# A two-layer hybrid trunk: TensorE keeps the order of the source over the sixteen RWKV units

## The chip, the core and the metric

The kernel runs on one core of a Trainium2 chip. A core has five engines, each with a queue of its own that it works off in order: TensorE (PE in the tables, its weight loads PEld), VectorE (DVE), ScalarE (ACT), GpSimd (POOL) and SyncE (SP), which issues most of the DMAs. The metric is the device time of one execution in microseconds. The kernel before took 1853.83 us, the median of three runs (1851.74, 1853.83 and 1856.85).

## The reference

One step of a trunk with two layers over 128 context tokens and 256 latent tokens, 384 in all, of width 1024, in float32. Layer 0 mixes with a Mamba-2 (SSD) head group beside an RWKV-7 head group, layer 1 with gated linear attention beside an mLSTM group. A squared-ReLU MLP follows each. What matters here is layer 0: one input projection feeds both groups, and RWKV-7 scans each of 16 heads in two directions:

```
s_kk = einsum('bhvk,bhk->bhv', s, kk_t)
s = s * exp(lw_t)[:, :, None, :] - s_kk[..., None] * (kk_t * a_t)[:, :, None, :] + v_t[..., None] * k_t[:, :, None, :]
y = einsum('bhvk,bhk->bhv', s, r_t)
...
out = concatenate([y_ssd, y_rw], axis=-1) @ p['w_out']
```

The kernel computes this scan by chunks of 64 tokens: per chunk a triangular 64x64 matrix is inverted, and a chain over the chunks carries the state.

## The kernel before, in words

**Units and slots.** Two heads share the 128 partitions (64 rows each), so there are eight pairs of heads, and with two directions sixteen RWKV units. `ab_streams` (line 1527) runs through 19 slots `s`. In slot `s` the unit `s` is prepared (`rw_prep`: the product `psc` of `KR` and `BK`, six matmuls at a time; and once per pair `rw_shared`: `pn`, `pw`, `pa`, `pst`), unit `s-1` is inverted (`rw_tokmajor` with `pv`, `pbk` and the product named `pr` that reads `UV,Q`, then `rw_inverse`), and unit `s-2` runs its chain (`rw_chain`: four rounds of `pr` <- `S,KR`, then `pu`, then `pd` and `py`). Beside them run the SSD head group's steps (`aux`) and the fill: the dense input projection (`dps`, three float32r matmuls per 128 rows of weights, split into a high part `wH` by ACT and a low part `wL` by DVE) and pieces of the conditioning map (`mod`, four matmuls that each use 32 columns of the array, so that four fit beside each other).

**Round trips.** A matmul writes PSUM; ACT or DVE brings the result to SBUF; only then can a next matmul read it. `rw_inverse` (line 1279) is a string of such trips: five times `pz`, then ACT copies it to `Zb`, then `pw` and `pt` read `Zb`, then DVE makes the new `W` and `T` from them, then the next `pz` reads `T`. At the end `pe` reads the last `T`, a last `pt` transposes `T`, ACT copies that to `W`, and `pc` reads it. `rw_chain` (line 1373) has `pr`, DVE `R`, `pu`, ACT and DVE `UV`, `pd`, DVE `S`, and again `pr`.

**What sets the order.** Each of these parts is a Python generator that yields where a round trip begins. `run` (line 1584) draws them in turn by a share of steps done, so the source order already lays other work between the two ends of a trip: a fill step is two blocks of 128 rows, six `dps` matmuls. That source order was then only a priority. A scheduler went over the whole program with its own idea of how long each instruction takes, and put next on each engine the first instruction, by source order, that it held to be ready. Where it held the next matmul in source order not to be ready, it took a later one instead.

**PSUM.** `dps` and `aux` have one bank each in this loop, the preparation's tiles and `mod` share two banks in turn, the inverse has two, the chain one, and `py` one.

Names that the change and the rows touch: line 221 issues every matmul, line 1266 the transposes `pbk`, lines 235 and 239 DVE's operations, line 277 ACT's copies.

Of the kernel before, what the change touches and what calls it, by code (L numbers as in the profile page):

```python
# [175 lines left out]
class Net:  # L176
# [1350 lines left out]
    def ab_streams(self):  # L1527

        NB = 16
        sh, us, fills = self.sh, self.us, self.fills  # L1530
        st = [dict() for _ in range(NB)]
        py = {}
        self.steps.update({"set": 7, "fill0": 37, "fill1": 24, "fill2": 15, "fill3": 14, "fill14": 16, "fill15": 32, "fill16": 30,
                           "fill17": 29, "ssd1": 11, "ssd2": 6, "ssd3": 9, "prep0": 12, "prep1": 9, "inv": 17, "tail": 3})
        for s in range(NB + 3):
            self.one_acc = s < NB
            self.lpool = LPOOL.get(s, 0)
            if s == 1:

                row = lambda: self.mpool.tile([128, T], F32, tag="nt", name="prow", bufs=2)[:, 0:128]  # L1540
                self.params_tr(self.params_in(range(3, self.params.shape[1] // 128), row, self.nc.sync))
            streams = []
            b = s - 2
            if 0 <= b < NB:
                j, d = divmod(b, 2)
                if d == 0:
                    py[j] = self.psy.tile([128, 512], F32, tag="y", name="py")
                streams.append(("chain", self.rw_chain(j, d, st[b], py[j], sh[j])))
            b = s - 1
            if 0 <= b < NB:  # L1550
                streams.append(("inv", self.seq(self.rw_tokmajor(b % 2, sh[b // 2], st[b]), self.rw_inverse(b % 2, st[b]))))
            b = s
            if b < NB:
                j, d = divmod(b, 2)
                prep = self.rw_prep(j, d, sh[j], st[b])
                if d == 0:
                    streams.append(("prep0", self.seq(self.rw_shared(j, sh[j]), prep)))
                else:
                    streams.append(("prep1", self.seq(prep, self.rw_bonus(j, sh[j]))))
            if s >= 4 and s % 2 == 0 and (s - 4) // 2 < 8:  # L1560
                j = (s - 4) // 2
                streams.insert(0, ("tail", self.rw_tail(j, sh[j], sh[j]["y"])))
            q, g = s % 4, s // 4
            if s < NB and q:
                if q == 1:
                    core = self.ssd_core(g, us[g])
                streams.append(("ssd%d" % q, self.part(core, SSD_PARTS[q])))
            if s == 0:
                streams.append(("set", self.set))
            if fills[s]:  # L1570
                streams.append(("fill%d" % (q if 0 < s < NB - 2 else s), self.pipe(fills[s])))
            self.run(streams)
        return sh[7]["y"]

    def part(self, gen, n):
# [1004 lines left out]
```

## Time and profile before

| | |
|---|---|
| device time, three runs | 1851.74, 1853.83, 1856.85 us |
| profiled execution | 1853.32 us, of it 1851.2 us from the first to the last instruction |
| PE busy | 1765.5 us (95%), 13661 matmul records |
| PEld busy | 1480.9 us (80%) |
| DVE busy | 1301.8 us (70%) |
| ACT busy | 1069.6 us (58%) |
| mean granted TensorE clock | 0.98 of 2.4 GHz |

The loop in question takes the stretch from about 88 us to 870 us. The first chain reaches its state output (`pf`) at 175 us and the sixteenth at 828 us, so fifteen units lie in 652.8 us. A float32 matmul shows as two records in the trace, a float32r or float16 matmul as one. A matmul's row tells start and duration, but matmuls overlap in the array, so what one costs is read from its start to the start of the next. Rows of one kind that follow each other are merged, with their number behind an x.

### The profile page before, as it was taken

How to read it: one execution, taken by the hardware profiler on the slowest of the kernel's cores; microseconds unless marked ns; L12 is line 12 of the kernel's file. 1: busy time of each engine (PE TensorE's matmuls, PEld its weight loads, DVE VectorE, ACT ScalarE, POOL GpSimd, SP SyncE). 2: the span in 40 equal slices, each digit the busy share in tenths (PEclk: the TensorE clock that was granted, in tenths of full speed). 3: DMA queues.
4: the chain of work that ended last, by engine and by line, in shares of the span. 5: the costliest groups of instructions: out<-in, count | busy, mean ns of one | idle time of the engine just before them, and what ended most of it. 6: DMA issues, size and time to landing. Idle time of an engine off the chain costs nothing.

```text
span 1851.2 us, 37384 instructions
## 1 busy us (share of the span) xinstructions
PE 1765.5 (95%) x13661; PEld 1480.9 (80%) x13661; DVE 1301.8 (70%) x2992; ACT 1069.6 (58%) x2688; POOL 216.6 (12%) x270
## 2 busy tenths in 40 slices
PE   7879999999999999999999999899999998999998
PEld 3667767766666677786999998889989897999887
DVE  3698788777878889758766334786786958766434
ACT  3567475746574777646655333777676756755322
POOL 3222111110112011101000000020211212000000
PEclk9889999999999999999999999999999998999999
DMA  8332443333334322345445643333333233344432
GB/s 280 112 88 65 123 133 97 106 87 112 102 105 126 101 65 81 100 119 175 117 124 171 177 146 101 102 91 102 102 94 92 74 108 106 115 125 126 150 134 80
DMA packets 314107, 213.55 MB, mean 115 GB/s; under 512 B 39648, under 2 KB 297494, under 8 KB 313924
## 3 DMA queue, kind: packets, MB, share of 16 engines
q1 hardware_dynamic: 308756, 208.35, 38.6%
q10 hardware_dynamic: 4816, 2.69, 0.5%
q8 instruction: 107, 1.75, 0.4%
q14 instruction: 76, 0.62, 0.1%
q0 software_dynamic: 352, 0.13, 0.0%
HBM read 201.32 MB, written 9.78 MB: 114 GB/s over the span
## 4 chain that ended last, share of the span: by engine, by line
PE 75%; DVE 10%; ACT 8%; DMA 4%; issue 2%; POOL 1%; SPq 0%; DVEq 0%; ACTq 0%; POOLq 0%
PE dps L221 45%; PE o L221 7%; PE ps L221 4%; PE mod L221 3%; PE aux L221 2%; DVE wL L235 2%; PE psc L221 2%; DMA raw<-in_w_mod 2%; PE py L221 1%; PE pt L221 1%; DVE cacc L242 1%; PE pr L221 1%; ACT wH L277 1%; PE pw L221 1%; ACT Zb L277 1%
## 5 line engine op out<-in xcount | busy, mean ns | idle before, releaser
L277 ACT ACTIVATE wH<-raw 128x256 fp32r<-128x256 f32 (+1 forms) x790 | 363.3, 480 | 429.3 <-PE dps L221 309.6
L235 DVE TENSOR_TENSOR wL<-raw,wH 128x256 fp32r<-128x256 f32 (+2 forms) x771 | 398.9, 536 | 243.2 <-ACT wH L277 239.5
L277 ACT ACTIVATE Zb<-pz 64x384 f16<-64x384 f32 x160 | 77.2, 483 | 36.4 <-PE pz L221 34.1
L242 DVE SCALAR_TENSOR_TENSOR cacc<-rows,params,cacc 128x384 f32<-128x384 f32 (+1 forms) x192 | 94.2, 491 | 0.7
L221 PE MATMUL dps<-sH,wH 128*128 128x384 f32 x232 | 85.8, 371 | 4.0 <-DVE m L235 3.5
L221 PE MATMUL dps<-sL,wH 128*128 128x384 f32 x232 | 80.5, 347 | 0.3 <-DVE sL L235 0.2
L221 PE MATMUL dps<-sH,wL 128*128 128x384 f32 x232 | 79.7, 345 | 0.5 <-DVE wL L235 0.5
L221 PE MATMUL dps<-h0H,wH 128*128 128x384 f32 (+1 forms) x147 | 58.9, 401 | 8.2 <-ACT h0H L277 3.5
L235 DVE TENSOR_TENSOR AO<-AHb,rwmask 128x768 f16<-128x768 f16 (+1 forms) x112 | 60.1, 537 | 7.7 <-PE pz L221 6.0
L235 POOL TENSOR_TENSOR BK<-BK,kkk 128x768 f32<-128x768 f32 x16 | 33.8, 2110 | 221.5 <-DVE BK L239 150.5
L221 PE MATMUL mod<-xT,cond 128*32 128x384 f32 (+1 forms) x320 | 55.2, 485 | 3.8 <-DVE Q L235 2.5
L221 PE MATMUL dps<-h6H,wH 128*128 128x384 f32 (+2 forms) x147 | 54.9, 373 | 2.7 <-ACT wH L277 2.7
L221 PE MATMUL dps<-h2H,wH 128*128 128x384 f32 (+1 forms) x147 | 55.6, 378 | 1.4 <-ACT wH L277 1.4
L221 PE MATMUL dps<-h4H,wH 128*128 128x384 f32 (+1 forms) x147 | 54.9, 378 | 2.1 <-ACT h4H L245 2.1
L235 POOL TENSOR_TENSOR gDb<-gb 128x384 f32<-128x384 f32 x28 | 33.2, 1187 | 173.5 <-DVE gb L2230 73.2
L221 PE MATMUL dps<-h1H,wH 128*128 128x384 f32 (+1 forms) x147 | 52.0, 354 | 0.0
L221 PE MATMUL dps<-h6H,wL 128*128 128x384 f32 (+2 forms) x147 | 50.8, 346 | 1.2 <-DVE wL L235 1.2
L221 PE MATMUL dps<-h0H,wL 128*128 128x384 f32 (+1 forms) x147 | 51.7, 351 | 0.0
L221 PE MATMUL dps<-h1H,wL 128*128 128x384 f32 (+1 forms) x147 | 51.6, 351 | 0.0
L221 PE MATMUL dps<-h0L,wH 128*128 128x384 f32 (+1 forms) x147 | 51.5, 356 | 0.0
L221 PE MATMUL dps<-h1L,wH 128*128 128x384 f32 (+1 forms) x147 | 51.3, 355 | 0.0
L221 PE MATMUL dps<-h2H,wL 128*128 128x384 f32 (+1 forms) x147 | 51.1, 348 | 0.0
(1163 smaller groups left out, 5450.0 us busy)
## 6 DMA issues: line engine op xcount, KB each, us to landing
raw<-in_w_mlp_up SPq DMA_DIRECT2D x64, 512.0 KB
raw<-in_w_mlp_down SPq DMA_DIRECT2D x64, 512.0 KB
raw<-in_w_in_ab SPq DMA_DIRECT2D x204, 128.0 KB
xT<-in_w_mod SPq DMA_DIRECT2D x128, 192.0 KB
raw<-in_w_in_cd SPq DMA_DIRECT2D x192, 128.0 KB
raw<-in_w_mod SPq DMA_DIRECT2D x64, 192.0 KB
raw<-in_w_mod SPq DMA_DIRECT2D x32, 256.0 KB
raw<-in_w_out_cd SPq DMA_DIRECT2D x64, 128.0 KB
```

What stands on the lines that cost most here:

```text
L221: self.nc.tensor.matmul(out, lhsT, rhs, start=start, stop=stop)
L235: return (eng or self.nc.vector).tensor_tensor(out=out, in0=a, in1=b, op=op)
L242: self.nc.vector.scalar_tensor_tensor(out=out, in0=a, scalar=s, in1=b, op0=op0, op1=op1)
L277: self.nc.scalar.activation(out=out, in_=in_, func=AF.Copy)
```

## The change

The call of `run` in `ab_streams` is put into a context in which the scheduler keeps TensorE's instructions in the order in which the source issues them. The other engines' instructions are still ordered by the scheduler, and so are TensorE's before and behind this loop. No instruction is added or taken away: both programs have 11552 matmuls and 2640 explicit weight loads.

```
             if fills[s]:
                 streams.append(("fill%d" % (q if 0 < s < NB - 2 else s), self.pipe(fills[s])))
-            self.run(streams)
+            with self.tc.manual_schedule(engines={mybir.EngineType.PE}):
+                self.run(streams)
         return sh[7]["y"]
```

What moves is shown at two places of slot 11. The first is TensorE before, from the end of a `pt` group of the inverse (before, this stretch ran at 596 to 603 us). `xT_9111` to `xT_9117` are the four pieces of one `mod` step.

```order
L221 MATMUL pr<-S,KR 64x64 x2
L221 MATMUL dps<-h0H,wL 128x384
L221 MATMUL dps<-h1H,wH 128x384
L221 MATMUL dps<-h1L,wH 128x384
L221 MATMUL mod<-xT_9111,cond 32x384
L221 MATMUL mod<-xT_9113,cond 32x384
L221 MATMUL pb<-t_9192,const_base 128x384
L221 MATMUL mod<-xT_9115,cond 32x384
L221 MATMUL dps<-h1H,wL 128x384
L221 MATMUL dps<-h2H,wH 128x384
L221 MATMUL dps<-h2L,wH 128x384
L221 MATMUL mod<-xT_9117,cond 32x384
```

TensorE in the changed kernel at the same place, behind the same `pt` group; the first `pz` is the next product of the inverse.

```order
L221 MATMUL pr<-S,KR 64x64 x2
L221 LDWEIGHTS AO_793
L221 MATMUL pz<-T,AO_793 128x64
...
L221 MATMUL mod<-xT_9146,cond 32x384
L221 MATMUL mod<-xT_9148,cond 32x384
L221 MATMUL mod<-xT_9150,cond 32x384
L221 MATMUL mod<-xT_9152,cond 32x384
L221 MATMUL pu<-R,WF 64x64 x2
```

The four `mod` now stand together, where before `pb` and `dps` stood between them. The ten `dps` that stood between the `pt` group and `pz` are gone from there and come later, so `pz` follows `pt` with one `pr` group between.

The second place is a little later on TensorE, before: behind `pc`, the last product of the inverse, with `pbk` of the next unit.

```order
L221 MATMUL pc<-W,AO 64x64
L1266 MATMUL pbk<-const_base,BK 128x64 x6
L221 MATMUL mod<-xT_9221,cond 32x384
L1266 MATMUL pbk<-const_base,BK 128x64 x6
L221 MATMUL pr_9367<-UV,Q 64x64 x12
L221 MATMUL pu<-R,WF 64x64 x2
L221 MATMUL pu<-R_8641,WF 64x64 x2
L221 MATMUL mod<-xT_9223,cond 32x384
L221 MATMUL mod<-xT_9225,cond 32x384
L221 MATMUL mod<-xT_9227,cond 32x384
```

And TensorE in the changed kernel.

```order
L221 MATMUL pc<-W,AO 64x64
L1266 MATMUL pbk<-const_base,BK 128x64 x12
L221 MATMUL pr<-S,KR 64x64 x2
L221 MATMUL dps<-h2H,wH 128x384
L221 MATMUL dps<-h2L,wH 128x384
L221 MATMUL dps<-h2H,wL 128x384
L221 MATMUL dps<-h3H,wH 128x384
L221 MATMUL dps<-h3L,wH 128x384
L221 MATMUL dps<-h3H,wL 128x384
L221 MATMUL pr_9405<-UV,Q 64x64 x12
```

The twelve `pbk` are whole again, and the `dps` come by six.

Counted over both programs as runs of matmuls of one kind and shape that follow each other: `dps` 455 before and 378 now; `mod` 101 and 82; `psc` 47 and 36; `pbk` 28 and 17; all kinds together 1905 and 1714.

## Rows read from the trace of the kernel before

**Rows 1.** The page, its first line on busy time and a costly group.

```profile
PE 1765.5 (95%) x13661; PEld 1480.9 (80%) x13661; DVE 1301.8 (70%) x2992; ACT 1069.6 (58%) x2688; POOL 216.6 (12%) x270
...
L235 DVE TENSOR_TENSOR wL<-raw,wH 128x256 fp32r<-128x256 f32 (+2 forms) x771 | 398.9, 536 | 243.2 <-ACT wH L277 239.5
```

**Rows 2.** Windows: length; busy of PE, PEld, DVE, ACT, POOL; PEclk, DMA share, GB/s.

```profile
175.30:219.00 43.70, 43.22 (x501) 31.36 (x500) 34.88 (x90) 24.42 (x67) 7.18 (x6) 1.00 0.41 117
...
788.10:828.10 40.00, 39.49 (x364) 33.35 (x361) 23.38 (x60) 15.98 (x41) 4.50 (x6) 1.00 0.42 120
sum 652.80, PE 632.60 PEld 462.90 DVE 522.53 ACT 399.77 POOL 90.72; mean PE 42.17 PEld 30.86 DVE 34.84 ACT 26.65 POOL 6.05
```

**Rows 3.** Timeline of PE (start, duration): a `dps` run broken by `pr`.

```profile
502.54 0.45 PE L221 MATMUL dps<-h6H,wH 128*128 128x384 f32 x1
502.92 0.33 PE L221 MATMUL pr<-S,KR 64*64 64x64 f32 x4
503.18 0.44 PE L221 MATMUL dps<-h6L,wH 128*128 128x384 f32 x1
503.46 0.34 PE L221 MATMUL dps<-h6H,wL 128*128 128x384 f32 x1
503.63 0.34 PE L221 MATMUL dps<-h7H,wH 128*128 128x384 f32 x1
```

**Rows 4.** Timeline of PE: one `mod` alone, and four together.

```profile
505.22 0.83 PE L221 MATMUL mod<-xT,cond 128*32 128x384 f32 x2
505.98 0.38 PE L221 MATMUL pt<-Zb,W 64*64 64x64 f16 x12
...
521.70 0.85 PE L221 MATMUL mod<-xT,cond 128*32 128x384 f32 x8 [0.41 <-ACT lw L245]
522.48 0.48 PE L221 MATMUL aux<-vw,bt 128*128 128x256 f32 x1
```

**Rows 5.** Timeline of PE: `psc` in a half group and whole.

```profile
552.35 0.93 PE L221 MATMUL psc<-KR,BK 64*128 64x128 f32 x6
553.21 0.45 PE L221 MATMUL dps<-h1H,wH 128*128 128x384 f32 x1
...
584.94 0.94 PE L221 MATMUL psc<-KR,BK 64*128 64x128 f32 x12
585.81 0.44 PE L221 MATMUL dps<-h4H,wH 128*128 128x384 f32 x1
```

**Rows 6.** Timeline of PE: `pbk` in a half group and whole.

```profile
511.32 0.58 PE L1266 MATMUL pbk<-const_base,BK 64*128 64x64 f32 x6
511.83 0.33 PE L221 MATMUL pr<-S,KR 64*64 64x64 f32 x4
...
560.39 0.59 PE L1266 MATMUL pbk<-const_base,BK 64*128 64x64 f32 x12
560.91 0.44 PE L221 MATMUL dps<-h4H,wH 128*128 128x384 f32 x1
```

**Rows 7.** Timeline of PE and DVE: the trip from `pt` over `T` to `pz`.

```profile
709.21 0.38 PE L221 MATMUL pt<-Zb,W 64*64 64x64 f16 x12
...
709.79 0.55 DVE L235 TENSOR_TENSOR T<-T,pt 128x384 f16<-128x384 f16 x1
...
710.56 0.35 PE L221 MATMUL pz<-T,AO 128*128 128x64 f16 x6
```

**Rows 8.** Timeline of PE: the trip from `pz` over `Zb` to `pw`.

```profile
707.51 0.34 PE L221 MATMUL pz<-T,AO 128*128 128x64 f16 x6
...
708.93 0.26 PE L221 MATMUL pw<-W,Zb 128*128 128x64 f16 x3 [0.41 <-ACT Zb L277]
```

**Rows 9.** Waits of PE from 175.3 to 828.1 us: total, times, longest.

```profile
PE pz L221 <- DVE T L235: 3.0, 5, 0.9
PE mod L221 <- DVE Q L235: 2.5, 3, 1.5
```

**Rows 10.** Windows, as in rows 2: the stretch with a low clock.

```profile
400.00:420.00 20.00, 18.50 (x150) 11.60 (x150) 13.67 (x34) 7.00 (x21) 4.08 (x5) 0.75 0.33 90
```

## Prediction

> **What bounds the kernel now.** I read the busy times first, then the windows of the loop, then TensorE's timeline inside it, and its waits last. TensorE is busy 95% of the span, the next engine, DVE, 70% [rows 1]. The change touches only the loop over the units, so the windows between the chains' state outputs matter: fifteen units in 652.8 us, 43.5 us each, with TensorE busy 632.6 us and DVE 522.5 us [rows 2]. TensorE is idle for 652.8 - 632.6 = 20.2 us in all of them, 1.3 us per unit. It waits for hardly anything: its waits for `T`, the most frequent kind in the inverse, come to 3.0 us in five cases, and the longest wait listed is 1.5 us [rows 9]. So the loop's time is what TensorE's instructions take in their order. That order is what changes.
>
> The timeline then shows that "busy" hides something. What a group costs depends on whether it is whole. One `mod` alone holds the engine from 505.22 to 505.98, 0.76 us; four of them, on four strips of the array, from 521.70 to 522.48, 0.78 us [rows 4]. So a group of four that is broken in two costs twice as much. Three `psc` (six records) take 0.86 us and six 0.87 us [rows 5]; six `pbk` take 0.51 us and twelve 0.52 us [rows 6]. A `dps` in a run takes 0.17 us from start to start, but the first of a run 0.28 us, and one that stands alone before a 64-row matmul 0.38 us [rows 3].
>
> **What the change gives: groups made whole.** The scheduler of before cut groups apart when it held a piece not to be ready; the source issues them whole. Counted over both orders, runs of one kind fall from 1905 to 1714, 191 fewer. Priced kind by kind:
>
> - `mod`: 19 runs fewer. Fourteen are 384 columns wide, 14 x 0.76 = 10.6 us. Five are 256 wide; at two thirds that is an estimate of 5 x 0.51 = 2.6 us. Together 13.2 us.
> - `dps`: 77 runs fewer, each saving at least the dearer first one, 0.28 - 0.17 = 0.11 us: 8.5 us. If each is also left for a 64-row matmul it is 0.38 - 0.17 = 0.21 us, or 16 us.
> - `psc`: 11 fewer. Before, seven groups are cut into three and three, at 0.86 us: 6.0 us. The four other cuts are of two and four and stand under the rest.
> - `pbk`: 11 fewer at 0.51 us: 5.6 us.
> - The rest: 191 - 77 - 19 - 7 - 11 = 77 runs (`py`, `pu`, `pr`, `pt`, `pw`, `aux`, `pa`). No row prices each. The lower bound is the 0.11 us of a `dps` run, the upper the 0.51 us of a `pbk` group. I take 0.18 us, near the first, since most of them are short: 14 us.
>
> Sum 13.2 + 8.5 + 6.0 + 5.6 + 14 = 47 us of TensorE's time, 2.9 us per unit. Could it be worth nothing? Only where a piece filled a time in which TensorE would have stood still, and the rows show 20.2 us idle in 652.8 in spite of the filling. With `dps` at 0.21 us and the rest at 0.51 us it would be 47 + 7.7 + 25 = 80 us. I stay with 47, since the rows for the large kinds are exact.
>
> **What the change takes: trips that lose their cover.** In source order a matmul that isn't ready holds all behind it. I matched in both orders each matmul with the one its operand comes from over ACT or DVE, and added up the TensorE work that stands between, at the prices above. The inverse has 240 such trips (over `Zb`, `T` and the last `W`). Those with less than 0.8 us of work between them are 8 before and 35 now. In the chain, the trips over `S` with less than 1.07 us go from 0 to 7. That is 34 more that will wait. The order shows why: at the end of an odd slot the fill has run out, `pz` stands right behind `pt`, and `pc` right behind the transposes it needs.
>
> What one costs: from the first `pt` at 709.21 to the `pz` at 710.56 it is 1.35 us with DVE going to `T` almost at once, and 0.38 us of that is the `pt` rows themselves [rows 7]. From `pz` at 707.51 to `pw` at 708.93 it is 1.42 us, and there the profile names `Zb` as what PE waited for [rows 8]. With some 0.4 us of other work between, one lacks 0.6 to 1.0 us. At the cheap end it is 0.5 us (a trip of 0.8 us cover, or one covered by the wait just before it): 34 x 0.5 = 17 us. At the dear end `T` stands behind two `wL` of 0.54 us each [rows 1], so 0.7 + 1.1 = 1.8 us: 34 x 1.8 = 61 us. I take 0.8 us, as DVE is busy 80% of the loop and some queueing is sure: 34 x 0.8 = 27 us.
>
> TensorE's clock adds to it. Before, the granted clock is 0.75 over 400 to 420 us [rows 10], that is part of the time at 1.2 instead of 2.4 GHz, and TensorE's longest wait of the loop, 1.5 us for `Q`, fell in that stretch just before. It cost 0.25 x 20 = 5 us. The new waits come two and three together in an odd slot, so this will happen again somewhere; I allow 3 us, between nothing and one case in each of four slots (20 us).
>
> **Sum.** -47 + 27 + 3 = -17 us. Against the profiled execution's 1853.3 us that is 1836 us. The profiled execution lies within 0.5 us of the median of the runs, 1853.83 us, so the same holds against the median: -0.96%. What lies outside the loop keeps its order and is put at nothing. DVE, ACT and SP get other orders as well, since the scheduler fits them to TensorE's; I put this at nothing because DVE has 652.8 - 522.5 = 130 us free in the loop. If that cover is gone it shows as the second rival.
>
> A rule that speaks against the change: the Trainium skill, "TensorE: Matmul & The Clock Gate", section "Part 3: Packing small matmuls — row/col tiling", says that matmuls start and end strictly in program order and only weight loads are pulled ahead. By that a matmul that waits can't be passed by the `dps` behind it, and each of the 34 short trips is paid in full; without it the 27 us would vanish. The trace agrees where it shows a wait: `mod` at 521.70 begins after 0.41 us of idle and the `aux` behind it starts only after it [rows 4].
>
> **Rivals.**
>
> *All of the 47 us comes through.* Waits that follow each other cover each other: a stop for `T` gives `UV` of the chain time to be ready. The order puts the new short trips together in some seven units, which speaks for it. Then 12 us of waits remain: 1853 - 35 = 1818 us.
>
> *DVE is the second bound, and nothing changes.* For it: DVE is busy 34.8 of 43.5 us in a unit [rows 2], every second operand comes from it, and it splits the weights. If TensorE becomes faster only to wait for `wL` and `T`, the idle time grows by what the groups save. Against it: TensorE waited for DVE hardly at all before [rows 9]. Then 1851 us. The Trainium skill, "Perfetto Trace Analysis", section "Identifying the Most-Contended Engine", would make this the forecast: it holds matmul busy time to be no good measure and wants the share of weight loads instead. By it TensorE stands at 462.9 of 652.8 us, 71%, under DVE's 80%. The trace agrees that busy hides reserve (the `mod` rows), but not that the engine waits.
>
> *Slower.* The place is the inverse in the odd slots, behind the last fill step. Every wait holds back the `dps` behind it too, so weight buffers come free later, ACT and DVE get their splits in a burst after the wait, and the next `T` queues behind them. The price is the dear end, 61 us, with 3 us of clock: -47 + 61 + 3 = +17, or 1870 us. It decides from 44 / 34 = 1.3 us a trip. For it: the scheduler put fill into these very places, and without it the trips of 1.35 us are bare. Against it: the deferred `dps` are not lost and stand behind as cover for the next unit.
>
> That the change does not do what it says is excluded by the orders: runs of `mod` and `pbk` are whole.
>
> **How the numbers follow.** Forecast 1836 us: 0.42, with a range of its own from 1824 to 1847 (47 us of groups, 17 to 35 us of waits and clock). All comes through, 1818 us: 0.20. No change, 1851 us: 0.15. Slower, 1870 us: 0.23. A measurement of this kernel can tell 0.3%, 5.6 us, from no change, so faster is under 1848 us and slower over 1859 us. Faster 0.42 + 0.20 = 0.62, same 0.15, slower 0.23. The range that should hold the time 8 times in 10 leaves out the outer half of the first rival (0.1) and the outer half of the slower one (0.1): 1814 to 1868 us.
>
> **What would show it.** In the profile after: the number of matmul records is the same, but `mod` rows come as x8 alone and `pbk` as x12. The fifteen units take 636 us instead of 652.8, with TensorE busy about 47 us less (586) and idle about 50 us instead of 20. The waits of PE list `pz` <- `T`, `pt` and `pw` <- `Zb` and `pc` <- `W` with totals of 5 to 10 us each where the first was 3.0. If busy time falls by much less than 47 us the pricing of the groups is wrong. If idle time grows by more than 47 us, trips cost over 1.3 us each and the sign turns. If the waits are mostly for `wL` or `wH` instead, DVE was the bound.

## The result, and the profile after

The changed kernel takes 1921.32 us, the median of four runs (1912.87 to 1924.42), against 1852.78 us before: 1.036 times, with a 95% interval from 1.0322 to 1.0398. It is slower by 68.5 us. The forecast was 1836 us, and 1868 us was the top of its range. Of the runs below, one of the kernel with source order in the odd slots (4063 us) and one of the kernel before in the last series (2710 us) were disturbed executions, and medians and ratios leave them out.

The first line on busy time and the clock by slices, from the page of the kernel after, answer to [rows 1].

```profile
PE 1758.5 (91%) x13661; PEld 1492.3 (78%) x13661; DVE 1310.4 (68%) x2992; ACT 1075.5 (56%) x2688; POOL 216.7 (11%) x270
...
PEclk9987998998899899979999999999999999999999
```

The number of matmul records is the same, and TensorE's busy time is 7.0 us less in a span that is 71.4 us longer. The clock is under full speed in several of the first twenty slices, those of the loop.

The windows between the chains' state outputs answer to [rows 2]: first unit, the slowest unit, the last, and the sum of fifteen. Below it is the same stretch taken as one window, where the column behind POOL is the mean granted clock.

```profile
191.30:234.30 43.00, 40.72 (x497) 30.35 (x494) 33.12 (x83) 23.22 (x65) 6.31 (x6) 1.00 0.40 114
...
431.80:492.10 60.30, 51.22 (x493) 37.44 (x490) 41.69 (x105) 33.63 (x85) 6.21 (x6) 0.77 0.29 84
...
849.90:897.80 47.90, 42.97 (x367) 36.62 (x364) 22.42 (x59) 16.59 (x41) 4.42 (x6) 0.89 0.35 102
sum 706.50, PE 625.71 PEld 474.16 DVE 528.00 ACT 402.34 POOL 90.76; mean PE 41.71 PEld 31.61 DVE 35.20 ACT 26.82 POOL 6.05
...
191.30:897.80 706.50, 625.71 (x7042) 474.16 (x7039) 528.00 (x1304) 402.34 (x1019) 90.76 (x98) 0.93 0.33 95
```

```profile
175.30:828.10 652.80, 632.60 (x7048) 462.90 (x7047) 522.53 (x1311) 399.77 (x1022) 90.72 (x98) 0.99 0.36 103
```

The second fence is the kernel before in one window. Fifteen units take 706.5 us instead of 652.8, which is 53.7 us more. TensorE is idle for 706.5 - 625.7 = 80.8 us instead of 20.2. Idle time alone grew by 60.6 us, more than the whole, and busy time fell by only 6.9 us. The clock says why it fell so little. A mean of 0.93, with levels of 0.5 and 1, means 0.07 x 2 x 706.5 = 99 us at 1.2 GHz; before it was 0.01 x 2 x 652.8 = 13 us. To separate the two I gave every matmul its start-to-start price from the trace of before, by kind and place in its run, and compared that with what it took. At those prices the fifteen units are 590.8 us of work before and 549.5 after, 41.3 us less. At half clock, matmuls worth 49.9 us took 90.3 us after, and 7.2 us took 13.3 before, so the clock costs 40.4 instead of 6.1 us. The account closes: -41.3 for the groups, +60.6 idle, +34.3 for the clock, which is +53.6 us. It closes as a difference only: in each kernel some 36 us of busy time are in none of these prices (632.6 - 6.1 - 590.8 and 625.7 - 40.4 - 549.5). Without any price, with half of what matmuls took at half clock put down to the clock (45.2 and 6.7 us), busy time less the clock falls by 45 us. The stretch before the first state output grew too, from 175.3 to 191.3 us. Of these 16.0 us own work is -3.1, idle time +13.8 (29.9 to 43.7 us) and the rest, the clock above all, +5.3. Behind the last one 1.7 us came on top.

What TensorE waits for in the fifteen units, after (total, cases, longest), answers to [rows 9].

```profile
PE pw L221 <- ACT Zb L277: 12.2, 11, 2.5
PE pz L221 <- DVE T L235: 10.3, 10, 2.5
PE pr L221 <- ACT fo L277: 8.4, 14, 0.8
PE pr L221 <- DVE S L235: 7.6, 6, 2.3
PE mod L221 <- DVE Q L235: 6.1, 7, 1.6
PE dps L221 <- ACT rows L277: 5.1, 2, 3.1
PE pbk L1266 <- DVE WF L235: 4.4, 5, 1.0
...
PE pc L221 <- ACT W L277: 2.5, 4, 0.7
...
PE pt L221 <- ACT Zb L277: 0.9, 3, 0.3
```

There are two kinds of rows here. `pw` and `pt` read `Zb`, `pz` reads `T`, `pr` reads `S` and `pc` reads `W`: these are the round trips, 34 waits with 33.5 us. But `pr` does not read `fo`, nor `mod` `Q`, nor `dps` `rows`, nor `pbk` `WF`. There the instruction named is the one that empties the PSUM bank into which the matmul will write: 28 waits with 24.0 us. Before, the same fifteen units have 7.1 us of the first kind in twelve waits (`pz` in [rows 9] and the two rows below, of the kernel before) and 3.0 us of the second, 2.5 of them for `Q`. The scheduler let other work pass such a matmul; source order can't.

```profile
PE pw L221 <- ACT Zb L277: 3.1, 5, 1.3
...
PE pt L221 <- ACT Zb L277: 1.0, 2, 0.6
```

One trip in TensorE's timeline after (start, duration; in brackets the idle time before it), and DVE's timeline in the same place.

```profile
638.97 0.35 PE L221 MATMUL pw<-W,Zb 128*128 128x64 f16 x6
639.25 0.37 PE L221 MATMUL pt<-Zb,W 64*64 64x64 f16 x12
639.46 0.31 PE L221 MATMUL pr<-S,KR 64*64 64x64 f32 x4
642.29 0.48 PE L221 MATMUL pz<-T,AO 128*128 128x64 f16 x6 [2.53 <-DVE T L235]
642.70 1.51 PE L221 MATMUL mod<-xT,cond 128*32 128x384 f32 x8
```

```profile
639.25 0.41 DVE L242 SCALAR_TENSOR_TENSOR cacc<-rows,params,cacc 128x192 f32<-128x192 f32 x1
639.58 0.28 DVE L235 TENSOR_TENSOR Z<-Z,yt 128x128 f32<-128x128 f32 x1
...
640.90 0.41 DVE L242 SCALAR_TENSOR_TENSOR cacc<-rows,params,cacc 128x192 f32<-128x192 f32 x1
641.23 0.55 DVE L235 TENSOR_TENSOR W<-W,pw 128x384 f16<-128x384 f16 x1
641.69 0.54 DVE L235 TENSOR_TENSOR T<-T,pt 128x384 f16<-128x384 f16 x1
```

This is the place that the forecast's first order block shows: `pz` with one `pr` group between it and the `pt` it depends on. DVE has other work queued, starts `T` at 641.69, and TensorE stands for 2.53 us. The `mod` group behind it is whole (x8), as forecast, but it comes at half clock: eight records take 644.14 - 642.70 = 1.44 us to the next start, where a whole group before took 0.78 us [rows 4].

### The profile page after: what moved, and what is told of

The parts are those of the page before. It is cut to its first block, busy times and chain, and to the rows that moved or that the text cites. A ratio compares the mean times of both kernels' runs of the same rounds, so it can differ in the third digit from the quotient of the medians.

```text
span 1922.6 us, 37408 instructions
## 1 busy us (share of the span) xinstructions
PE 1758.5 (91%) x13661; PEld 1492.3 (78%) x13661; DVE 1310.4 (68%) x2992; ACT 1075.5 (56%) x2688; POOL 216.7 (11%) x270
## 4 chain that ended last, share of the span: by engine, by line
PE 60%; DVE 9%; ACT 6%; DMA 2%; issue 2%; POOL 0%; SPq 0%; DVEq 0%; ACTq 0%; POOLq 0%
PE dps L221 38%; PE o L221 7%; PE ps L221 4%; DVE wL L235 1%; PE mod L221 1%; PE aux L221 1%; DVE cacc L242 1%; PE ms L221 1%; ACT wH L277 1%; PE pr L221 1%; PE py L221 1%; ACT Zb L277 1%; DMA raw<-in_w_mod 1%; DVE acc L235 1%; DVE AO L235 1%
## 5 line engine op out<-in xcount | busy, mean ns | idle before, releaser
L235 DVE TENSOR_TENSOR wL<-raw,wH 128x256 fp32r<-128x256 f32 (+2 forms) x771 | 403.8, 542 | 267.8 <-ACT wH L277 263.2
L221 PEld LDWEIGHTS <-AO 128*128 128x128 f16 (+1 forms) x672 | 27.3, 105 | 34.1 <-issue 27.1
L235 DVE TENSOR_TENSOR W<-W,pw 128x384 f16<-128x384 f16 x64 | 35.1, 549 | 26.8 <-PE pw L221 26.6
L221 PEld LDWEIGHTS dps<-sH,wH 128*128 128x128 f32 x232 | 44.5, 192 | 11.5 <-issue 5.4
L221 PEld LDWEIGHTS dps<-h0H,wH 128*128 128x128 f32 x147 | 28.5, 194 | 31.8 <-ACT rows L277 11.9
```

What stands on the lines that cost most here:

```text
L221: self.nc.tensor.matmul(out, lhsT, rhs, start=start, stop=stop)
L235: return (eng or self.nc.vector).tensor_tensor(out=out, in0=a, in1=b, op=op)
```

## The experiments

Each is timed beside the kernel before, whose medians are 1851.5 to 1855.4 us. "Source order" stands for TensorE in the order of the source.

**The group price alone.** Under the scheduler, as before, with the `mod` pieces issued in reverse:

```
-            for g, w in enumerate(raw):
+            for g, w in reversed(list(enumerate(raw))):
```

> The kernel before, all under the scheduler, with the four pieces of a mod step issued last first. That alone makes the scheduler leave most of them together: runs of mod fall from 101 to 83, all runs from 1905 to 1880, and short covers stay as few as before. If broken groups cost what the forecast priced (0.76 us a lone mod of 384 columns, 0.51 us one of 256), 10 to 13 us go: 1841 to 1844 us. Rival: a broken group costs nothing, because TensorE gives the time back in waits for DVE, and the 47 us of the forecast were never there: 1851 to 1856 us.

1836.83 us, ratio 0.991 (0.9881 to 0.994): 16.7 us less, more than expected. The fifteen units of this kernel, as one window:

```profile
174.10:809.10 635.00, 612.32 (x7049) 457.63 (x7047) 521.98 (x1311) 399.42 (x1022) 90.27 (x98) 1.00 0.38 106
```

They are 17.8 us shorter, though idle time is no less (22.7 us, before 20.2): 9.5 us is own work by the prices, and 6.1 us is the clock, which is at full speed throughout. Less the 2.5 us of idle time that is 13.1 us, and 4.7 us are not accounted for. The group price is real, and the gain does not need source order. This kernel beats both.

**A bank wait taken away.** Source order, with the state output in the preparation's two banks:

```
-                pf = self.psc("pf")
+                pf = self.psp("pf")
```

> The changed kernel with the chain's state output pf put into the two banks of the preparation instead of the chain's one bank. The trace after lists 14 waits of the next pr for fo, the copy that empties that bank, 8.4 us together. If waits for a bank are lost time of TensorE, these go: 1911 to 1914 us; if they also pulled the clock down, 1903 to 1911. Rival: such a wait only stands in for the wait for S or T that comes next, and the time stays at 1919 to 1924 us.

1913.69 us, ratio 1.0328 (1.0311 to 1.0345); against the changed kernel 7.6 us less by the medians, though the intervals overlap. In its waits, whose first four rows follow, `fo` is gone:

```profile
PE pw L221 <- ACT Zb L277: 13.7, 12, 2.5
PE pz L221 <- DVE T L235: 13.0, 11, 2.5
PE pr L221 <- DVE S L235: 7.5, 7, 2.3
PE mod L221 <- DVE Q L235: 6.1, 7, 1.6
```

Idle time in fifteen units fell by 6.4 us only (80.8 to 74.4), and `T` and `Zb` are waited for 4.2 us longer, which suggests that some of the bank wait was cover for the next trip. The expected 8 us for the wait alone came about, the larger gain with the clock did not, though the time at half clock fell from 99.0 to 88.7 us. This kernel is the base of what follows, named e2.

**Where in the loop.** Source order in the odd slots only, in the even slots only, and from slot 4 on (here with `pf` as in the changed kernel). For the odd slots:

```
-            with self.tc.manual_schedule(engines={mybir.EngineType.PE}):
+            with self.tc.manual_schedule(engines={mybir.EngineType.PE}) if s % 2 == 1 else ExitStack():
```

> Source order on TensorE in the odd slots only, the scheduler's in the even ones. The forecast's slower rival put the loss into the odd slots, where the fill runs out before the inverse ends: then nearly the whole loss is here, 1900 to 1920 us. Theory now: the loss sits wherever a matmul stands right behind the one it depends on, through a copy or through a bank, in both kinds of slot, and counted over the orders the even slots have more of such places (28.7 us of missing cover in fifteen units against 16.0): 1865 to 1880 us here.

1883.38 us, the median of three, ratio 1.0163 (1.0146 to 1.018).

> Source order on TensorE in the even slots only. If the loss sits in the odd slots, this keeps the gain of whole groups without the waits: 1835 to 1850 us. If it sits in both, and more in the even ones (missing cover 28.7 us in fifteen units, and all of slot 0, which begins the loop): 1885 to 1905 us.

1899.96 us, ratio 1.0248 (1.023 to 1.0266). The two losses, 29.9 and 46.4 us, add up to somewhat more than the whole 68.5. The even slots lose 16.6 us more than the odd ones, as the theory had it (the odd ones came out 3 us above its window). But 10.0 us of the even slots' loss arise before the first state output, which comes at 185.3 instead of 175.3 us: slot 0 is an even one. The odd slots are not the place, and the later even ones are at most a little worse.

> Source order on TensorE only from slot 4 on; slots 0 to 3 and all before stay with the scheduler. Theory: the first state output came 16 us later in the changed kernel (191.3 against 175.3 us), which the forecast did not price, and that part goes, with the second unit's start: 1901 to 1909 us. Rival: the later slots only wait longer for what the first ones left undone: 1917 to 1925 us.

1902.19 us, ratio 1.0257 (1.0221 to 1.0292): 19 us less than the changed kernel. Its first state output comes at 174.5 us again, and the fifteen units behind it take 698.2 us. The first stretch is a loss of its own.

**The clock behind the waits.** e2 with matmuls that do nothing useful in 37 waits of TensorE (a table `PAD` gives the number for each group):

```
+    def pad(self, name, p):
+        k = self.padn[name] = self.padn.get(name, -1) + 1
+        for _ in range(PAD.get((name, k), 0)):
+            self.mm(p[:, 0:128], self.c("mean"), self.c("ident"))
```

> The kernel of e2_pf_bank with extra matmuls whose result is overwritten at once: 188 of a constant 128x128 by a constant of 128 columns, put before the 37 groups of pz, pw, pc and pr for which e2's trace shows TensorE idle for over 0.4 us because the copy of their operand is late (43.5 us in all), each group getting as many as fit its wait. They give TensorE something to do in the wait and can't shorten it. Theory: a good part of the loss is the clock at 1.2 GHz that follows such waits (in the fifteen units of e2, 43.8 us of work at full speed took 86.2 us, with 5.9 idle, so 36 us lost). Then the time at half clock falls to less than half and the time from 1913.7 to 1888 to 1903 us, although more work is done. Rival: the low clock has another cause, or costs nothing since the copies are waited for anyway; then 1914 to 1930 us, the extra matmuls costing what the waits do not cover.

1913.41 us, ratio 1.0314 (1.0289 to 1.0338), no different from e2. So the next one had smaller pieces, `self.mm(p[:, 0:128], self.i128h, self.i128h)`.

> As e5_fill_waits, but in smaller pieces, so that they fit: 520 float16 matmuls of a constant 128x128 by 128 columns, before the same 37 groups of the kernel of e2_pf_bank, each group as many as leave 0.3 us of its wait free (at 0.06 us each, 31 us in all). In e5 the time at half clock fell, but the extra work (32 us in fifteen units) was larger than the idle time it took up (25 us). Theory (the low clock behind the waits costs time of its own): with extra work that stays inside the waits the gain shows in the time, 8 to 16 us off e2's 1913.7: 1898 to 1906 us. Rival (what the clock gives back is waited for again at the next operand): 1910 to 1918 us.

1907.11 us, ratio 1.0292 (1.0271 to 1.0313): 6.6 us less than e2, short of the theory's 8 to 16 and outside the rival's window too. Fifteen units of e2, e5 and e8:

```profile
191.90:888.80 696.90, 622.54 (x7042) 472.87 (x7039) 525.00 (x1304) 401.83 (x1019) 91.10 (x98) 0.94 0.34 97
```

```profile
188.40:884.50 696.10, 646.31 (x7357) 498.91 (x7355) 525.95 (x1306) 402.11 (x1020) 90.36 (x98) 0.96 0.34 97
```

```profile
185.70:877.90 692.20, 637.90 (x7481) 489.47 (x7478) 525.83 (x1306) 402.43 (x1020) 91.06 (x98) 0.96 0.34 98
```

The clock rises from 0.94 to 0.96 in both, though nothing else was done than to give TensorE work at its waits. From the clock's records the time at half clock is 88.7 us in e2, 51.2 in e5 and 58.0 in e8. In e8 the extra matmuls take 32.3 us from start to start and idle time falls from 74.4 to 54.3, 20.1 us; the whole falls by 4.7. So all other matmuls became 4.7 + 32.3 - 20.1 = 16.9 us shorter: that is about what the clock gives back (half of the 30.7 us less at half clock is 15.4). Of it 12.2 us is spent again, as the extra matmuls take that much more than the idle time that went. The trace of e8 shows where:

```profile
623.68 0.55 DVE L245 TENSOR_TENSOR T<-T,pt 128x384 f16<-128x384 f16 x1
623.82 3.71 PE L225 MATMUL pz<-i128h 128*128 128x128 f16 x37 [2.07 <-DVE W L245]
...
627.37 0.34 PE L225 MATMUL pz<-T,AO 128*128 128x64 f16 x6
```

The extra matmuls write into the bank of the group behind them, so they stand in the same wait until `W` has emptied it, 2.07 us here, and then run on: `T` is there at 624.23, and `pz` starts at 627.37. From the end of the operand to the start of its group, less what a plain wait shows there (0.05 us for `pz` and `pw`, 0.14 for `pr`), the groups with extra matmuls come 10.7 us late in e8's fifteen units, 9.0 of it in four of the 31 places, and some 18 us in e5's. So most of what e8 did not gain was lost by its own extra work. That a faster clock shortens the cover of the next trip, the rival's reading, is not shown. An estimate of what filled waits give without the overrun is 4.7 + 10.7 = 15 us in fifteen units, inside the theory's 8 to 16. What e5 and e8 show is that the waits bring the clock down.

**The trips themselves.** e2, with the copies and subtractions of the inverse's five levels reading a constant instead of `pz`, `pw` and `pt` (three edits of this kind, and two `Zb` in turn):

```
-                self.acopy(Zb[h, :, h], zv[h])
+                self.acopy(Zb[h, :, h], self.Fc[h])
...
-            self.tt(f(T2), f(Tm), pt[:, :T], ALU.subtract)
+            self.tt(T2, Tm, self.Fc, ALU.subtract)
```

> The kernel of e2_pf_bank (source order) without the round trips of the inverse's five levels: the copies to Zb and the subtractions that make W and T are made as before, but read a constant instead of pz, pw and pt, and Zb has two tiles in turn. All matmuls are issued in nearly the same order (1715 runs, 551 us of own work in fifteen units against 549.5), ACT and DVE have as many instructions; what is left out is the use of the products pz, pw and pt, so the output isn't the reference's. In e2 TensorE's waits for T and Zb from 80 to 890 us come to 35 us (pz 15.1, pw 17.7, pt 2). Theory (these uncovered trips, with the clock behind them, are the largest part of the loss): 33 to 50 us go, 1864 to 1881 us. Rival (the next wait takes their place, as DVE's or a bank's): 1893 to 1912 us.

1871.26 us, ratio 1.0096 (1.0062 to 1.0131): 42.4 us less than e2, in the middle of the theory's window. Its waits and its fifteen units:

```profile
PE pr L221 <- DVE S L235: 10.6, 8, 2.3
PE mod L221 <- DVE Q L235: 5.1, 7, 1.3
PE ps L221 <- DVE modsb L235: 4.1, 2, 2.3
PE pbk L1266 <- DVE WF L235: 4.0, 5, 1.0
```

```profile
181.10:843.50 662.40, 607.98 (x7040) 460.23 (x7040) 527.21 (x1306) 403.66 (x1021) 94.42 (x98) 0.97 0.36 102
```

Idle time falls by 20 us (74.4 to 54.4) and busy time by 14.6 us, as the time at half clock falls from 88.7 to 41.0 us. What is left is the chain's trip over `S`, the wait for `modsb` and the banks. The control, with the same edits on the kernel before:

> The control of e11_trips_cut: the kernel before, all under the scheduler, with the same five levels cut from their trips in the same way (the products pz, pw and pt are not used, so the output isn't the reference's). The scheduler's order changes a little with it: runs fall from 1905 to 1857, own work in fifteen units from 591 to 581 us. The waits for T and Zb are 6 us here. Theory: before, the trips are covered, so what goes is the 9 us of groups and at most the 6 us of waits: 1837 to 1848 us, and the gap between source order and scheduler falls from 60 us (e2 against before) to 20 to 40. Rival (trips cost both kernels alike, and the loss lies elsewhere): 1800 to 1825 us.

1850.57 us, ratio 0.9986 (0.997 to 1.0001), 3 us above the theory's window and far from the rival's. So 60 us between e2 and before become 21 us, which would make two thirds of e2's loss the inverse's uncovered trips with the clock behind them. But the control has a loss of its own. The 9 us of groups did not show, since its time at half clock is 41.0 us, as in e11, against 13.7 in the kernel before. Half of that time, 20.5 us from 287.8 on, begins inside the longest wait of its fifteen units, one of the chain:

```profile
288.66 0.48 PE L221 MATMUL pr<-S,KR 64*64 64x64 f32 x4 [2.57 <-DVE S L235]
```

Half of the 27.3 us more is an estimate of what this cost, 13.7 us. Without it the gap would be 34 us, and the trips' share 26 of 60. So between two fifths and two thirds of what e2 loses are the inverse's uncovered trips with the clock behind them; a few waits more or less in the control move it that far.

**Two ideas to mend it, both wrong.** First a fill step of one block instead of two (`self.grain = 1`), on e2.

> The kernel of e2_pf_bank with a fill step of one block of 128 rows (three dps) instead of two, so that the source lays dps between more pairs of dependent matmuls. Runs of one kind rise from 1714 to 1828, TensorE's own work in fifteen units by 13 us (549 to 562), and the missing cover counted over the order falls from 25 to 21 us in fifteen units and from 12 to 6 in the first stretch. Theory (waits and the clock behind them are the loss): 1895 to 1908 us. Rival (the price of broken groups weighs more): 1915 to 1928 us.

1943.28 us, ratio 1.0477 (1.0453 to 1.05), worse than either. The fifteen units take 23 us longer than e2's: 13 us more own work, as counted, 9 us of clock, and idle time the same. Its first two rows of waits:

```profile
PE pw L221 <- ACT Zb L277: 17.5, 20, 1.8
PE pz L221 <- DVE T L235: 7.1, 12, 1.7
```

`pw` waits 20 times instead of 12. Three `dps` are 0.51 us of cover [rows 3] for a trip from `pz` to `Zb` that takes 1.2 us at the least (1.28 in the median); two blocks cover most of one, so the finer step leaves more trips short, each by less. My count of missing cover had charged one of `Zb`'s two copies, 0.48 us, where ACT makes them one behind the other.

Then the second of those copies on DVE.

```
-            for h in halves:
-                self.acopy(Zb[h, :, h], zv[h])
+            self.acopy(Zb[halves[0], :, halves[0]], zv[halves[0]])
+            self.nc.vector.tensor_copy(Zb[halves[1], :, halves[1]], zv[halves[1]])
```

> The kernel of e2_pf_bank with the second of Zb's two copies on DVE instead of ACT. In e2's trace the trip from the last pz to Zb takes 1.28 us in the median, because ACT makes both copies, 0.48 us each, one behind the other; before, it was as long, but covered. If the trip's own length is the loss, about 0.4 us goes from each of some 12 waits of pw for Zb (13.7 us) and of 5 of pt, with the clock behind them: 1899 to 1908 us. Rival: DVE, which has the T, W and wL to make, is late with its half, or T is later by as much: 1911 to 1925 us.

1936.47 us, ratio 1.0457 (1.0426 to 1.0489): the rival's way, and beyond its window.

```profile
PE pw L221 <- DVE Zb L1334: 18.8, 17, 2.6
PE pz L221 <- DVE T L235: 16.3, 12, 3.0
PE pr L221 <- DVE S L235: 10.9, 6, 4.2
```

In e2 these rows were 13.7, 13.0 and 7.5. One copy of `Zb`, `T` and `S` now stand in one queue.

**Whose queue?** DVE, and then DVE and ACT, in the order of the source too (on e2): `engines={mybir.EngineType.PE, mybir.EngineType.DVE}`, and with `Activation` as a third.

> The kernel of e2_pf_bank with DVE in the order of the source too in the loop; TensorE's order stays nearly the same (1717 runs against 1714). If the queue that the scheduler made on DVE is what makes the uncovered trips long, T and S come as early as their place in the source, the waits for them (20 us in e2's fifteen units) fall by half or more, and with the clock 12 to 25 us go: 1888 to 1902 us. Rival: a DVE that may not pass an operand that isn't there stands still itself, and makes all others late: 1925 us or more. If neither matters, 1908 to 1920 us.

1998.79 us, ratio 1.0816 (1.0767 to 1.0866).

> The same with ACT in the order of the source as well. By the queue theory the waits for Zb (14 us in e2's fifteen units) fall too: 1875 to 1895 us. By the rival each engine stands at the first operand that is late, and the copies that empty TensorE's banks come later: 1930 us or more.

2105.18 us, ratio 1.1377 (1.1339 to 1.1414). TensorE's first two waits in the first, and what DVE itself waits for there:

```profile
PE pz L221 <- DVE T L235: 29.8, 16, 5.5
PE pt L221 <- DVE W L235: 22.2, 13, 3.6
```

```profile
DVE wL L235 <- ACT wH L277: 28.1, 34, 3.0
DVE UV L239 <- PE pu L221: 25.3, 23, 3.3
DVE R L235 <- PE pr L221: 20.7, 17, 3.4
```

The queue theory falls. From the last `pt` to the end of `T` the slowest tenth of the trips took 2.2 us or more in e2 and 4.6 us here: a DVE that may not pass a late operand is later with everything. The scheduler's order on DVE and ACT was the better one for these trips.

**A second group kind under the scheduler.** e1 with `wL` first in each block of `dps`:

```
+                    self.mm(ps, lo[:, k, :], xh, start=first, stop=False)
                     first = False
-                    self.mm(ps, h[:, k, :], xl, start=False, stop=False)
...
```

> The kernel of e1_mod_whole (all under the scheduler, the mod pieces issued last first) with the three dps of a block issued with wL first, wH behind, so that a group starts only when its last operand is there. Runs of dps fall from 536 to 525 and of all kinds from 1880 to 1871; TensorE's own work in fifteen units from 581 to 579 us, and the covers stay. If the group price holds for dps too (0.11 to 0.21 us a run), 1 to 3 us off e1's 1836.8 in the loop: 1832 to 1836 us. Rival: wL is the operand that comes last, so waiting for it before the group starts costs cover everywhere dense work runs, the later layers too: 1840 to 1860 us.

1847.46 us, ratio 0.9964 (0.9946 to 0.9982): the rival's window, 10.6 us worse than e1. Its loop takes 643.0 us instead of 635.0, with the clock at 0.98 instead of 1.00, idle time up by 2.8 us, and `pw` waiting for `Zb` 3.9 us (8 cases) instead of 1.9 (4). Eleven runs of `dps` saved 2.6 us of own work by the prices, and lost more.

## Why the prediction was wrong, step by step

**Groups made whole, -47 us: right in sum.** The prices give -41.3 us in the fifteen units and -3.1 before them. The `mod` term is confirmed by itself in e1, where 18 runs of `mod` fewer made 16.7 us, of which 6 are the clock. How the rest divides among the other kinds is not shown by a run.

**Uncovered trips, 34 x 0.8 = 27 us: nearly right.** Besides the 34 waits of 33.5 us there are seven in the first stretch (`pw` 4.1, `pz` 2.3, `pc` 0.6 us). That is 41 waits with 40.5 us, 0.99 us each; less the twelve with 7.1 us of before, 29 waits and 33.4 us more. e11 confirms that these trips matter, with 42 us when those of the inverse are cut, but some 15 us of that is the clock. A trip's own length did not grow: from the last `pz` to the second `Zb` it is 1.28 us in the median in both kernels, and the slowest tenth to the end of `T` was 2.8 us before and 2.1 after. So the new orders of ACT and DVE, which the forecast put at nothing, did not lengthen it; only the cover went. (The forecast called `T` the most frequent wait of the inverse; the rows above have `Zb` in seven cases against five.) By this step alone the change would still have been faster, -44 + 33.

**Waits for a bank: the step that was missing.** I matched operands only, so a matmul that waits for the emptying of the bank it writes had no term in the sum. These are 24.0 us in fifteen units, and 8 us in the first stretch (`dps` for `rows` 5.1, `psc` for `Q` 1.4, `pbk` for `WF` and `dps` for `k` 0.8 each); less some 4 us before, 28 us more. [Rows 9] held the hint: "mod <- DVE Q" is such a wait, and I read it only as a stop before the clock fell. e2 takes one kind away and gets 7.6 us by the medians; the other kinds were not taken away.

**Clock, 3 us: the step that failed most.** It is 34.3 us in the fifteen units, and about 40 us in all. I allowed between none and four falls, 20 us at most. After, there are 23 stretches at half clock between 88 and 870 us, and in the 5 us in front of each TensorE had stood idle for 1.2 to 3.7 us, in one wait or in a few close together. [Rows 10] had shown one such case, behind a wait of 1.5 us, and its price of 5 us; with 34 new waits expected, four falls was no upper bound. e5, e8 and e11 show that the falls follow the waits. Together: -44 for the groups, +33 for the trips, +28 for the banks, some 13 of other waits, and 40 of the clock are +70 us; with the 1.7 us behind the last state output that is the growth of the span, 71.4 us. The forecast's own range had a slip as well: 47 us of groups less 17 to 35 us of waits and clock gives 1823 to 1841 us, not 1824 to 1847.

**The first stretch: not looked at by itself.** 16 us of the sum above arise before the first state output, and e7 takes them back; one wait of 6.6 us (`aux` for `Y`) is among them.

**The rivals.** *Slower* was right in sign (1870 us foreseen), and its mechanism, waits that hold everything behind them while DVE's queue runs on, stands in the rows at 639 to 642 us. Its place was wrong: the odd slots alone lose 29.9 us, the even ones 46.4. Its point of decision, idle time that grows by more than 47 us, was passed (60.6 us). *All comes through* argued that waits cover each other. There may be something in it: e2 took 8.4 us of waits away and idle time fell by 6.4. It is far too little. *DVE is the second bound* fails as told: DVE's share of the fifteen units falls from 80% to 528.0 / 706.5 = 75%, and no row of TensorE's waits names `wL` or `wH`. The rule of the Trainium skill, "Perfetto Trace Analysis", section "Identifying the Most-Contended Engine", which judges TensorE by its share of peak arithmetic and of weight loads, would by the second have had DVE on top (474.2 / 706.5 = 67% here against 75%). The trace disagrees as to rate, while e9 shows that DVE's queue matters as delay, 22.8 us for 80 copies of 0.56 us. The rule of the Trainium skill, "TensorE: Matmul & The Clock Gate", section "Part 3: Packing small matmuls — row/col tiling", that matmuls keep program order agrees with the trace: nothing passes the `pz` at 642.29.

## What to carry to other kernels

An order that passes a late matmul costs something in broken groups, but it buys cover; when the order is to be fixed, price every wait that the scheduler stepped around, the waits for a PSUM bank among them, and add to each the clock that follows. Where group integrity is what is wanted, look for a local edit that makes the scheduler keep the group (here one `reversed`, 0.991) and leave it the rest. When a wait in the profile names a tile that the waiting instruction doesn't read, look for the buffer that the two share; in the rows above it was a PSUM bank. Work that is put into a wait must not itself stand in that wait: the extra matmuls of e8 needed the same bank.

## What the runs showed that was not expected

The scheduler's broken order was the better one each time that an engine more was fixed: in source order on TensorE alone the loss against the scheduler is 60 us (e2), with DVE 147, with DVE and ACT 254 us. And work that does nothing, put at waits, made the kernel 6.6 us faster by the medians (1913.69 to 1907.11), in spite of the 10.7 us by which it held the groups behind it back, while the time at half clock fell by 31 us; the two intervals just touch, so the 6.6 us itself is less sure than the clock.
